# Handing the multiplications of a 31-tap depthwise convolution from GpSimd to ScalarE

## The chip, the cores and the metric

The kernel runs on one core of one Trainium2 chip. The metric is the device time of one execution in microseconds (us). The program has five engines that work from queues of their own: TensorE (PE in the profile; PEld is its weight load), VectorE (DVE), ScalarE (ACT), GpSimd (POOL) and SyncE (SP, which issues the DMAs).

## The reference, cut to what matters

The model is a stack of two blocks. The second has two layers, each with a "hybrid mixer" that adds two branches. Branch a is a gated delta rule over 4 heads, forward and backward; branch b is a convolution branch:

```
u = cf_val * jax.nn.sigmoid(cf_glu)                            # 512 tokens x 512 channels
u = depthwise_conv_centred(u, cf_conv_w) + cf_conv_b           # 31 taps along the tokens, per channel
u = jax.nn.silu(layer_norm(u, cf_ln_w, cf_ln_b))
y_b = (u * jax.nn.silu(z_b)) @ w_cf_out
gate = jax.nn.sigmoid(gate_lg + gate_b).reshape(bsz, seq, N_BRANCH, D_MODEL)
y = gate[:, :, 0] * y_a + gate[:, :, 1] * y_b
return y @ w_out
```

All of it is float32. A token's output is a sum over 31 neighbours, each times a weight of its channel.

## The kernel before

Activations lie with channels on the 128 partitions and the 512 tokens along the free axis, one tile ("page") of 128x512 for each 128 channels. A GEMM tile is 8 steps k of three 128x512 matmuls each (lines 331, 334, 335: weights and activations are split into a high and a low part), and each weight tile is split first, by ScalarE (line 77, the high part) and VectorE (line 78, the low part).

The hybrid (line 1783) runs three kinds of work at once. The **foreground** is a row of GEMMs in program order: the projections of the four heads (`gdn_proj`), the convolution's input (`cf_proj`, which stores its four tiles `U` to DRAM), 16 gate tiles (line 1872), 4 tiles `zb` (line 1881), then `branch(1)`, which multiplies the convolution's result by `w_cf_out`. The **heads** (`gdn_head`, two at a time, background) are chains of small matmuls: an inverse (`CH.inverse`, lines 705 to 737, with a GpSimd copy at 718, a ScalarE copy at 730, a VectorE transpose at 729 and a VectorE subtraction at 736) and then 8 scan steps (lines 2096 to 2153). The **convolution** (`cf_conv`, background too) goes through the four channel tiles one after another.

What is woven with what is decided while the program is written out. The planner keeps a clock of its own, `K.now`. Each step k of a foreground GEMM calls `tick`, which moves the clock on by 3 x 512 / 2.37 = 648 ns and then lets those background strands emit that are due. A strand yields two numbers: a cost that moves the clock, and a wait, after which, times `LF` = 2.5, it is due again. The convolution yields `0, CVL` with `CVL` = 900, so that its next step is due 2250 ns later. Tile's scheduler then sets each engine's fixed order, with the order of emission as priority; an instruction can be put ahead of an earlier one where its data and its pages are there, except that foreground matmuls and the heads' matmuls are pinned to each other's order.

Two lines decide what follows the foreground (1884 and 1885): while the convolution has steps left, the planner lets the background strands run alone, and no GEMM is emitted.

```
    while any(s[1] is conv for s in K.back):
        K.wait()
    Yb = cf_norm(K, l, zb, U)
```

Behind them come `cf_norm` (layer norm, SiLU and the product with `zb`), `branch(1)` with the heads' remaining steps woven in, and `K.drain()` (line 1900), which again lets the heads run alone until they end. Then `branch(0)`, which needs all four heads, and `add_out`.

In `cf_conv`, a tile's centre tap and bias are one ScalarE instruction (line 1773). Of its 30 side taps, 20 are VectorE `scalar_tensor_tensor` instructions (line 1779: source times weight plus accumulator, all in SBUF). The other 10 (`PT`) go to GpSimd, each as two instructions: a multiplication into the page `x` (line 1945) and an addition into a second accumulator `g` (line 1946). VectorE adds the two accumulators at the end (line 1950).

Of the kernel before, what the change touches and what calls it, by code (L numbers as in the profile page):

```python
# [10 lines left out]
AF = mybir.ActivationFunctionType  # L11
# [3 lines left out]
ADD, SUB, MUL, MAX = ALU.add, ALU.subtract, ALU.mult, ALU.max  # L15
# [1728 lines left out]

CVL = 900
SLG = 1.0
PT = range(1, 31, 3)
HP = 10


# [15 lines left out]
def conv_n(K, dst, src, n, taps, bias=None, skip=()):  # L1766

    nc = K.nc
    c = len(taps) // 2
    if bias is None:  # L1770
        nc.scalar.activation(dst[:, :n], src[:, :n], AF.Copy, scale=taps[c])
    else:
        nc.scalar.activation(dst[:, :n], src[:, :n], AF.Identity, scale=taps[c], bias=bias)  # L1773
    for j in range(len(taps)):
        o = j - c
        if o == 0 or j in skip:
            continue
        a, b = max(0, -o), n - max(0, o)
        nc.vector.scalar_tensor_tensor(dst[:, a:b], src[:, a + o:b + o], taps[j], dst[:, a:b], MUL, ADD)  # L1779
        yield 0, CVL  # L1780


def hybrid(K, CH, l, X):
# [74 lines left out]
    for h in range(2):  # L1858
        proj(h)
        K.background(heads[h], head(h), slow=SLG)  # L1860
    cf_proj(K, l, X, w, U)
    conv = cf_conv(K, l, U)
    K.background(pro, conv)
    for h in range(2, 4):
# [65 lines left out]
def cf_conv(K, l, U):  # L1930

    nc = K.nc
    for t in range(4):
        while len(K.free_pages["p"]) < 4:
            yield 0, 1000
        src = K.load(U[t], "l")
        taps = [K.v(f"cfw{l}", 4 * j + t) for j in range(31)]
        U[t], g = [K.p2(name="cfa") for _ in range(2)]
        x = K.p2(name="tap")
        conv = conv_n(K, U[t], src, LT, taps, K.v(f"cfb{l}", t), PT)  # L1940
        nc.gpsimd.memset(g, 0.0)
        for j in PT:
            o = j - 15
            a, b = max(0, -o), LT - max(0, o)
            nc.gpsimd.tensor_scalar(x[:, a:b], src[:, a + o:b + o], taps[j], None, MUL)  # L1945
            nc.gpsimd.tensor_tensor(g[:, a:b], g[:, a:b], x[:, a:b], ADD)  # L1946
            for _ in range(2):
                yield next(conv, (0, CVL))
        yield from conv
        nc.vector.tensor_tensor(U[t], U[t], g, ADD)  # L1950
        K.free(src, g, x)


def cf_norm(K, l, zb, U):
# [335 lines left out]
```

## Time and profile before

| what | value |
|---|---|
| time, median of 3 runs | 3411.72 us (3407.67 to 3417.12) |
| profiled execution, its own time | 3407.66 us |
| its span, first to last instruction | 3406.0 us |
| mean granted TensorE clock | 0.958 |
| busy share PE / DVE / ACT / POOL | 93% / 62% / 37% / 18% |

The busy shares are means over the whole program; the two hybrid layers lie in about the last 1150 us of the span, and only there does the convolution run. The page's digits for POOL are near zero in most of the program and reach 5 of 10 in the hybrids.

### The profile page before, as it was taken

To read this page: it belongs to the slowest core of one execution; us is meant where nothing else is said; L and a number is where in the kernel's file an instruction comes from. 1 tells how busy PE (TensorE), PEld (TensorE's weight loads), DVE (VectorE), ACT (ScalarE), POOL (GpSimd) and SP (SyncE) were. 2 spreads that over 40 slices of the span, in tenths; PEclk is the share of its full clock that TensorE was granted. 3 is DMA by queue.
4 is the path that set the end of the run, shared out by engine and by line. 5 is a ranking of instruction groups with operands and counts; after the bars stand their busy time and mean duration, and the time that the engine had idled before them with its cause. 6 is when DMAs were issued, how large, how long until landed. Compare 5 with 4: busy or idle time off the path is not lost. (4 is left out here: it accounts for less than half of the span.)

```text
span 3406.0 us, 61963 instructions
## 1 busy us (share of the span) xinstructions
PE 3156.2 (93%) x25042; PEld 2473.4 (73%) x25042; DVE 2114.3 (62%) x4318; ACT 1271.8 (37%) x2681; POOL 624.0 (18%) x762
## 2 busy tenths in 40 slices
PE   7999988889899999989888999989999998899998
PEld 4878766667588888868766788857667676766756
DVE  4444556545855555584766675668578666777765
ACT  4333333333432222355534332352333335244332
POOL 4111223211000000010010000005158100515700
PEclk9999999999899999989999999989999898999989
DMA  7432545441222122222222233232223253223333
GB/s 233 137 94 71 166 148 166 133 124 51 76 72 69 64 79 66 77 66 71 87 66 87 87 100 123 87 100 72 72 90 100 76 174 95 75 69 100 100 118 105
DMA packets 313570, 336.10 MB, mean 99 GB/s; under 512 B 26542, under 2 KB 259132, under 8 KB 313284
## 3 DMA queue, kind: packets, MB, share of 16 engines
q1 hardware_dynamic: 311172, 329.69, 30.6%
q8 instruction: 197, 3.23, 0.4%
q0 software_dynamic: 2112, 2.45, 0.3%
q14 instruction: 89, 0.73, 0.1%
HBM read 282.13 MB, written 49.94 MB: 97 GB/s over the span
## 5 line engine op out<-in xcount | busy, mean ns | idle before, releaser
L331 PE MATMUL mm<-hl,wh 128*128 128x512 f32 (+1 forms) x3296 | 1252.2, 384 | 53.8 <-DVE qkv L1779 13.8
L334 PE MATMUL mm<-hl,wh 128*128 128x512 f32 (+1 forms) x3296 | 1223.6, 372 | 1.9 <-DVE hl L474 1.6
L335 PE MATMUL mm<-hl,wl 128*128 128x512 f32 (+1 forms) x3296 | 1215.9, 371 | 0.0
L331 PEld LDWEIGHTS mm<-hl,wh 128*128 128x128 f32 x3296 | 629.6, 192 | 194.8 <-issue 40.4
L335 PEld LDWEIGHTS mm<-hl,wl 128*128 128x128 f32 x3296 | 630.3, 191 | 114.0 <-issue 2.3
L334 PEld LDWEIGHTS mm<-hl,wh 128*128 128x128 f32 x3296 | 632.2, 192 | 104.9 <-DVE hl L474 4.0
L77 ACT ACTIVATE wh<-wr 128x512 fp32r<-128x512 f32 (+3 forms) x718 | 367.4, 561 | 698.1 <-PE mm L334 610.9
L78 DVE TENSOR_TENSOR wl<-wr,wh 128x512 fp32r<-128x512 f32 (+3 forms) x718 | 438.3, 644 | 213.6 <-ACT wh L77 196.8
L1357 DVE SCALAR_TENSOR_TENSOR cv<-mm,vecs,cv 128x441 f32<-128x441 f32 (+2 forms) x352 | 243.0, 692 | 94.2 <-ACT cv L1345 88.1
L1408 POOL MEMSET gwh<- 128x1024 f32 x3 | 2.9, 955 | 971.3 <-PE mm L334 971.3
L1779 DVE SCALAR_TENSOR_TENSOR cfa<-ld,vecs,cfa 128x497 f32<-128x497 f32 (+14 forms) x160 | 154.3, 964 | 18.3 <-ACT cfa L1773 16.1
L1945 POOL TENSOR_SCALAR tap<-ld,vecs 128x498 f32<-128x498 f32 (+4 forms) x80 | 150.7, 1883 | 46.7 <-DVE kq L2004 10.4
L1380 DVE TENSOR_TENSOR fy<-fy,mm 128x512 f32<-128x512 f32 x96 | 55.1, 576 | 126.3 <-PE mm L335 125.5
L1946 POOL TENSOR_TENSOR cfa<-cfa,tap 128x498 f32<-128x498 f32 (+4 forms) x80 | 113.0, 1413 | 5.3
L2121 ACT ACTIVATE u<-ps,beT 64x128 f32<-64x128 f32 x128 | 46.3, 362 | 137.1 <-DVE u L2120 136.1
L730 ACT ACTIVATE pad<-ps 128x256 f32<-128x256 f32 (+1 forms) x100 | 46.6, 467 | 129.9 <-PE ps L726 129.4
L1359 ACT ACTIVATE cv<-cv,vecs 128x256 f32<-128x256 f32 (+1 forms) x66 | 43.0, 653 | 132.1 <-DVE cv L1357 77.2
L736 DVE TENSOR_TENSOR cut<-cut,ps 128x256 f32<-128x256 f32 x120 | 49.4, 413 | 58.9 <-PE ps L735 57.2
L353 POOL TENSOR_TENSOR rs<-var,mhalf 128x4 f32<-128x4 f32 (+1 forms) x26 | 28.1, 1082 | 287.5 <-DVE var L351 287.4
L412 PE MATMUL ps<-sq,one 128*128 128x512 f32 (+1 forms) x132 | 64.5, 625 | 17.0 <-ACT sq L382 15.7
L1363 DVE TENSOR_TENSOR cv<-cv,mm 128x512 f32<-128x512 f32 x66 | 39.4, 599 | 65.5 <-ACT cv L1359 36.2
L2120 DVE TENSOR_SCALAR u<-ps,kdT 64x128 f32<-64x128 f32 x128 | 44.6, 348 | 52.9 <-PE ps L2116 44.5
(479 smaller groups left out, 4465.3 us busy)
## 6 DMA issues: line engine op xcount, KB each, us to landing
ar<-in_ada_w_dram SPq DMA_DIRECT2D x96, 512.0 KB
wr<-in_ffn_up_dram SPq DMA_DIRECT2D x44, 1024.0 KB
wr<-in_w_in_dram SPq DMA_DIRECT2D x28, 1024.0 KB
ld<-sp SPq DMA_DIRECT2D x84, 256.0 KB
wr<-in_w_in_dram SPq DMA_DIRECT2D x32, 512.0 KB
xsp<-x SPq DMA_DIRECT2D x48, 256.0 KB
x<-xsp SPq DMA_DIRECT2D x48, 256.0 KB
wr<-in_ffn_down_dram SPq DMA_DIRECT2D x20, 512.0 KB
```

The source lines that it names most:

```text
L77: nc.scalar.activation(h[:, q:e], src, AF.Copy)
L78: nc.vector.tensor_tensor(l[:, q:e], src, h[:, q:e].bitcast(F32), SUB)
L331: mm = nc.tensor.matmul(ps[:m, :n], wh[:, i, :m], H[:, :n], start=first and i == 0, stop=False)
L334: nc.tensor.matmul(ps[:m, :n], wh[:, i, :m], L[:, :n], start=False, stop=False)
L335: nc.tensor.matmul(ps[:m, :n], wl[:, i, :m], H[:, :n], start=False, stop=last and i == nk - 1)
L412: self.nc.tensor.matmul(ps[:, :n], self.one2, t[:, :n], start=first, stop=last)
L736: nc.vector.tensor_tensor(Wp, Wp, ps, SUB)
L1357: nc.vector.scalar_tensor_tensor(t3[:, ro, co], a3[:, ri, ci], tap(ky, kx, ff), t3[:, ro, co], MUL, ADD)
L1380: nc.vector.tensor_tensor(y[s][q], y[s][q], pss[s][:, :n], ADD)
L1779: nc.vector.scalar_tensor_tensor(dst[:, a:b], src[:, a + o:b + o], taps[j], dst[:, a:b], MUL, ADD)
L1945: nc.gpsimd.tensor_scalar(x[:, a:b], src[:, a + o:b + o], taps[j], None, MUL)
L1946: nc.gpsimd.tensor_tensor(g[:, a:b], g[:, a:b], x[:, a:b], ADD)
```

## The change

The set of taps on GpSimd's side becomes every second one, 16 of 30 instead of 10; VectorE keeps the other 14. For each of the 16, ScalarE multiplies (an activation with `Copy` and the weight as scale) into one of two pages used in turn, and GpSimd only adds. The inner loop yields once for each of the 16, where it yielded twice for each of 10. A tile needs five free pages to begin instead of four, since there is one page more for products.

```
-PT = range(1, 31, 3)
+PT = range(0, 31, 2)
...
-        while len(K.free_pages["p"]) < 4:
+        while len(K.free_pages["p"]) < 5:
...
-        x = K.p2(name="tap")
+        xs = [K.p2(name="tap") for _ in range(2)]
...
-        for j in PT:
+        for i, j in enumerate(PT):
             o = j - 15
             a, b = max(0, -o), LT - max(0, o)
-            nc.gpsimd.tensor_scalar(x[:, a:b], src[:, a + o:b + o], taps[j], None, MUL)
+            x = xs[i % 2]
+            nc.scalar.activation(x[:, a:b], src[:, a + o:b + o], AF.Copy, scale=taps[j])
             nc.gpsimd.tensor_tensor(g[:, a:b], g[:, a:b], x[:, a:b], ADD)
-            for _ in range(2):
-                yield next(conv, (0, CVL))
+            yield next(conv, (0, CVL))
...
-        K.free(src, g, x)
+        K.free(src, g, *xs)
```

## Rows read from the trace of the kernel before

**Rows 1.** The page's part 1: busy us, share of the span, instructions.

```profile
PE 3156.2 (93%) x25042; PEld 2473.4 (73%) x25042; DVE 2114.3 (62%) x4318; ACT 1271.8 (37%) x2681; POOL 624.0 (18%) x762
```

**Rows 2.** Busy time by stretch: length, each engine's busy us, PEclk, DMA share, GB/s.

```profile
2338.00:2390.00 52.00, 44.64 (x571) 35.73 (x571) 45.79 (x51) 12.58 (x22) 43.40 (x27) 0.93 0.14 42
2482.00:2522.00 40.00, 34.96 (x159) 22.97 (x159) 31.73 (x61) 11.01 (x26) 35.43 (x23) 0.91 0.18 60
2589.00:2649.00 60.00, 55.42 (x718) 42.48 (x717) 44.04 (x63) 17.69 (x35) 45.28 (x30) 1.00 0.27 85
2682.00:2711.60 29.60, 23.59 (x128) 14.22 (x127) 21.09 (x57) 13.08 (x35) 2.63 (x3) 0.60 0.22 67
2711.60:2752.60 41.00, 39.85 (x174) 28.02 (x173) 20.82 (x55) 10.02 (x30) 1.10 (x2) 0.96 0.63 207
3258.50:3287.50 29.00, 22.63 (x130) 13.99 (x130) 21.39 (x58) 13.42 (x36) 1.31 (x2) 0.65 0.23 70
```

**Rows 3.** The same stretches, line 331's instructions alone: PE, PEld, PEclk, DMA, GB/s.

```profile
2682.00:2711.60 29.60, 0.00 (x0) 0.00 (x0) 0.60 0.22 67
2711.60:2752.60 41.00, 17.95 (x41) 8.07 (x41) 0.96 0.63 207
3258.50:3287.50 29.00, 0.00 (x0) 0.00 (x0) 0.65 0.23 70
```

**Rows 4.** PE's timeline at the end of layer 0's last head.

```profile
2742.54 0.43 PE L2143 MATMUL ps<-u,at 64*64 64x128 f32 x2
...
2750.57 0.60 PE L2171 MATMUL ps<-ident,ot 128*128 128x128 f32 x4
```

**Rows 5.** Groups by line, hybrids: busy us, mean ns | idle before, releasers.

```profile
L1779 DVE SCALAR_TENSOR_TENSOR cfa<-ld,vecs,cfa 128x497 f32<-128x497 f32 (+14 forms) x160 | 154.3, 964 | 18.3 <-ACT cfa L1773 16.1
...
L1945 POOL TENSOR_SCALAR tap<-ld,vecs 128x498 f32<-128x498 f32 (+4 forms) x80 | 150.7, 1883 | 46.7 <-DVE kq L2004 10.4 <-PE mm L335 10.3 <-DMA sp<-gt 6.8
L1946 POOL TENSOR_TENSOR cfa<-cfa,tap 128x498 f32<-128x498 f32 (+4 forms) x80 | 113.0, 1413 | 5.3
L718 POOL TENSOR_TENSOR pad<-L,zm 128x512 f32<-128x512 f32 x40 | 59.2, 1485 | 62.3 <-PE ps L726 47.4 <-ACT L L2081 14.7
```

**Rows 6.** Line 1779 by its instructions: duration ns min/median/max, first and last start.

```profile
L1779 DVE SCALAR_TENSOR_TENSOR cfa<-ld,vecs,cfa x160: 695/745/1823, 2339.4 to 3193.0; 128x497 f32<-128x497 f32 x16, 128x500 f32<-128x500 f32 x16, 128x503 f32<-128x503 f32 x16, 128x506 f32<-128x506 f32 x16
L1779 DVE SCALAR_TENSOR_TENSOR qkv<-mm,vecs,qkv x96: 714/748/752, 2266.5 to 3057.3; 128x510 f32<-128x510 f32 x48, 128x511 f32<-128x511 f32 x48
```

**Rows 7.** DVE's timeline in layer 0's first and second tile: start, us.

```profile
2340.01 0.69 DVE L78 TENSOR_TENSOR wl<-wr,wh 128x512 fp32r<-128x512 f32 x1
2340.61 1.75 DVE L1779 SCALAR_TENSOR_TENSOR cfa<-ld,vecs,cfa 128x499 f32<-128x499 f32 x1
2342.28 1.77 DVE L78 TENSOR_TENSOR wl<-wr,wh 128x512 fp32r<-128x512 f32 x1
...
2486.06 1.53 DVE L1779 SCALAR_TENSOR_TENSOR cfa<-ld,vecs,cfa 128x506 f32<-128x506 f32 x2
```

**Rows 8.** POOL's timeline at the same two places, and its last tap of layer 0.

```profile
2340.29 1.54 POOL L1946 TENSOR_TENSOR cfa<-cfa,tap 128x498 f32<-128x498 f32 x1
2341.78 1.72 POOL L718 TENSOR_TENSOR pad<-L,zm 128x512 f32<-128x512 f32 x1
...
2485.08 1.86 POOL L1945 TENSOR_SCALAR tap<-ld,vecs 128x501 f32<-128x501 f32 x1
...
2647.67 1.26 POOL L1946 TENSOR_TENSOR cfa<-cfa,tap 128x499 f32<-128x499 f32 x1
```

**Rows 9.** DVE's weight splits of 128x512 in the hybrids, by form.

```profile
L78 DVE TENSOR_TENSOR wl<-wr,wh 128x512 fp32r<-128x512 f32 x204 | 157.4, 801 | 63.8 <-ACT wh L77 59.8 <-PE ps L2038 3.6
```

**Rows 10.** ACT's groups by form in the hybrids.

```profile
L1773 ACT ACTIVATE cfa<-ld,vecs,vecs 128x512 f32<-128x512 f32 x8 | 6.5, 816 | 19.9 <-DMA ld<-sp 13.3 <-DMA sp<-gt 5.1 <-DVE kq L2004 1.5
...
L382 ACT ACTIVATE sq<-cfa 128x512 f32<-128x512 f32 x8 | 4.6, 619 | 0.0
```

**Rows 11.** What PE waited for, 2335 to 2400 us: total, times, longest.

```profile
PE ps L726 <- DVE W L736: 7.4, 3, 5.3
```

## The prediction

> **What bounds the kernel now.** First the page's part 1 [rows 1]: TensorE is busy 93% of the span and GpSimd 18%. So time saved on GpSimd is worth nothing in itself; the question is where TensorE waits in the hybrids, and whether that wait hangs on the convolution. Second, busy time by stretch [rows 2]. The first three rows are three of the stretches in which GpSimd works on taps in layer 0: PE is idle 52.0 - 44.6 = 7.4, 5.0 and 4.6 us, 17 in sum, while DVE is busy 45.8 of 52, 31.7 of 40 and 44.0 of 60. Layer 1 repeats the code, so I count 34 us in two layers. The waits view names it in the first stretch [rows 11]: the inverse's matmul (726) waits for VectorE's subtraction (736), queued behind taps and weight splits. Third, the rows of 2682.0 to 2711.6 and 3258.5 to 3287.5: PE is busy 23.6 of 29.6 us at a granted clock of 0.60, and 22.6 of 29.0 at 0.65. Line 331 alone shows why [rows 3]: not one foreground matmul ran there. This is the planner's loop at lines 1884 and 1885: zb's GEMMs are out, the convolution has planned steps left, so only the heads run, on latencies. On the chip the convolution's last GpSimd tap starts at 2647.67 and takes 1.26 us [rows 8], so it is done 33 us before this hole begins: the hole comes from the written-out order, not from data. In full-clock work it holds 23.59 x 0.60 = 14.2 us, so 15.4 of 29.6 are lost; in layer 1, 22.63 x 0.65 = 14.7, so 14.3. Together **29.7 us** hang on when the planner thinks that the convolution ends.
>
> **The change part by part.** All counts are for two layers, eight tiles.
>
> *VectorE's taps.* 160 become 112. At their mean of 964 ns [rows 5] that is -46.3 us of VectorE; but the same instruction fed from PSUM, which never met GpSimd, takes 714 to 752 [rows 6]. At 741, inside that, 48 taps are -35.6; the other 223 ns x 160 = 35.7 us are something else.
>
> *That something else is GpSimd's addition.* A tap that starts 0.3 us into an addition takes 1.75 us, and the split behind it, which meets the copy of line 718, 1.77 [rows 7, 8]: each starts its real work when the two-input GpSimd instruction is through. Under a GpSimd multiplication (2485.08, 1.86 us) two taps took 1.53 together, 0.77 each: almost undisturbed. So it is the additions that cost VectorE, and these go from 80 to 128, while the harmless multiplications go. Measured per addition: 35.7 / 80 = 0.45 us of tap time. Bounds for one addition: nothing, where VectorE works from PSUM at that moment, and 1.75 - 0.74 = 1.0. I keep 0.45, the mean over all tiles: 128 x 0.45 = 57.6, against 35.7 now: +21.9. Splits pay too: 801 ns in the mean [rows 9] against 0.69 us for an undisturbed one [rows 7], 0.11 x 204 = 22 us over 120 two-input GpSimd instructions (80 additions, 40 copies); with 168 it is 9 more. VectorE in sum: -35.6 + 21.9 + 9 = **-5 us**, hardly a relief; with no further collision -36, with 1.0 for each addition about +66.
>
> The Trainium skill (SBUF — State Buffer, "Who interferes with whom") says that a VectorE instruction with two SBUF inputs contends with any GpSimd instruction that reads SBUF, and that the pair is locked for the whole instruction. The rows agree for additions and not for the one-input multiplication. By the rule the contention would follow GpSimd's whole tap time, which falls; that is a rival below.
>
> *GpSimd.* -80 x 1.883 = -150.7, +48 x 1.413 = +67.8: tap time 263.7 becomes 181 us, 22.6 a tile instead of 33 [rows 5]. Off the path; the 40 copies of line 718 that stand in the same queue get shorter waits, unless an addition ahead of them waits for its product.
>
> *ScalarE.* +128 multiplications, 128x497 and wider, from SBUF with a scale per partition. No such row: from below 619 ns (a square from SBUF, no scale), from above 816 (scale and bias per partition, from SBUF) [rows 10]. I take 0.70, nearer the square, since the bias falls away: +90 us (79 to 104), 11.2 a tile. Cover: ScalarE is busy 12.6 of 52, 11.0 of 40 and 17.7 of 60 in these stretches [rows 2]. What it costs all the same: each ScalarE instruction that meets a multiplication under way waits half of 0.70; with 11.2 us in about 40 that is 0.1 us apiece. These stretches hold 22 + 26 + 35 of them per layer, perhaps a quarter on a head's chain: 2 us a layer, **+4**. Bounds: 0, and 2 x 83 x 0.1 = 17. The new wait is that multiplication i+2 needs the page that addition i frees; behind it in ScalarE's queue stand the high splits (77), the copies 730 and the scan's u (2121). With additions at 1.4 us and products at 0.7 ScalarE is the faster one and would wait, if the order were not fixed with room between. No DMA is added; the loads of tiles 1 to 3 are only issued earlier.
>
> *Pages.* Five free instead of four. Followed through the code's bookkeeping, 14, 8, 10 and 9 pages are free where the tiles begin, so the gate costs nothing.
>
> *The planner.* The part that I think decides. Each layer now plans 4 x 20 = 80 convolution steps, at least 2.25 us apart, each rounded up to the next foreground step of 0.648 (half a step in the mean: 2.57): 206 us; stepped through, the code's clock gives 209. Foreground from the convolution's start to zb's end: 28 GEMM tiles x 8 x 0.648 = 145 us, plus the heads' own costs, 41 in that stretch: 186. The convolution outlasts it by 23, and that is the hole. After: 4 x 16 = 64 steps, 64 x 2.6 = 167 us, under 186. The loop has nothing to wait for; `branch(1)` follows zb directly and covers the heads' steps that now run alone. The heads are not shortened: what they have left then runs alone in the drain, two scan steps and the output of the last head. That costs, from rows: from the last scan matmul to the transposes 8.0 us [rows 4], and two steps at 29.6 / 5 = 5.9 (five steps of each head ran in the hole), 20 in sum. In it TensorE can do some 9 steps k of `branch(0)` that do not need the last heads: the second stretch has 41 [rows 3] where `branch(1)` has 32. They are 9 x 0.69 = 6.2 us; the steps' own matmuls are about 3. So 11 are lost there, where 15.4 + 41.0 - 39.85 x 0.96 = 18.1 are lost now: -7 in layer 0, -6 in layer 1 with its smaller hole, **-13**. Bounds: 0 (the hole moves whole) and -29.7.
>
> *When taps run.* The four tiles take 167 of planned time, not 209, so the inverse of heads 2 and 3 is about half clear of them (4.6 us idle in the third stretch: -2.3), and the scan's crowded stretch has 6 taps fewer of 20 (5.0 idle x 6/20 = -1.5). Two layers: **-8** (0 to -10, which is 34 x 6/20).
>
> Sum against the profile's own 3407.66 (span 3406.0 and 1.7 around it): -13 - 8 + 4 = -17, so 3390.7. The median stands 4.1 above that execution, so **3395** for it. VectorE's -5 is inside the -8.
>
> **The rivals.** (a) *The hole is only moved*: the heads alone at the end cost what they cost now, at a low clock. For it: their chain is unchanged. Then -8 + 4 remains: 3408, within the bound of 0.3% (10 us), about what these runs can tell from nothing. (b) *Additions crowd VectorE*: at 0.9 us each, which back-to-back additions make likely where VectorE is 88% busy already [rows 2], the taps cost 128 x 0.9 - 35.7 - 35.6 = +44 and the splits +9, 53 us of VectorE; if half reaches TensorE, 26 - 13 + 4 = +17: 3429, slower. It decides from a collision of 0.63, where half of 128 x 0.63 - 71.3 + 9 = 18 eats the 9 that hole and ScalarE leave. Against it: in the scan most VectorE operands come from PSUM. (c) *Contention falls with GpSimd's tap time*: if any GpSimd work on taps held VectorE up alike, collisions would be 35.7 x 181 / 263.7 = 24.5, so taps fall from 154.3 to 83 + 24.5 = 107.5, -30%; the 34 us of idle lose as much or a little more, 13, and the hole gives 20: 3383. Against it stand the undisturbed taps of [rows 7, 8]. It is what the section of the Trainium skill named above would give.
>
> **How the numbers follow.** Forecast 0.42 (3383 to 3405), (a) 0.20, (b) 0.25, (c) 0.13. Faster by over 0.3% (under 3401.5): most of the forecast, 0.36, all of (c), 0.02 of (a): 0.51. Slower: 0.25, from (b). Same: 0.24. The range takes in (c) and its bounds below and (b) above: 3374 to 3428.
>
> **What would show it.** Right: line 331 runs on past zb without the gap, a shorter gap stands ahead of `branch(0)`, line 1946 has 128 at 1.4 to 1.6 us, line 1779's taps a mean near 1.25, ScalarE's multiplications 0.62 to 0.82. Wrong: taps near 1.75 and longer waits of line 726 for 736 (b); a gap as long as now, elsewhere (a); taps under 1.0 (c); or idle time of ScalarE in front of the new line that ends with GpSimd, with splits and copies late behind it.

## The result: slower by 31 us, and the profile after

The changed kernel takes 3441.0 us (median of 6 runs, 3437.54 to 3452.2) against 3410.31 us for the kernel before (6 runs beside it, 3407.54 to 3417.12): ratio 1.0095, 95% interval 1.0078 to 1.0112. That is 31 us slower; 17 us faster was forecast.

The profiled execution of after has a span of 3450.5 us, 44.5 more than before's 3406.0. Of these, 9.7 stand ahead of the first hybrid layer, where the order is unchanged (its first `qkv` instruction comes at 2272.6 instead of 2262.9), so they are not the change's. Layer 0 is 18.8 longer (574.5 to 593.3 us from its first `qkv` to that of layer 1) and layer 1 16.0 (568.6 to 584.6, to the end).

The page's part 1 of after, as [rows 1]:

```profile
PE 3171.2 (92%) x25042; PEld 2480.6 (72%) x25042; DVE 2097.4 (61%) x4270; ACT 1357.2 (39%) x2810; POOL 537.2 (16%) x730
```

VectorE and GpSimd are both less busy than before (-16.9 and -86.8 us), and the kernel is slower: the sums can't tell why. The groups of after, as [rows 5] (busy us, mean ns | idle before, releasers); ScalarE's products are line 1946 now and GpSimd's additions line 1947:

```profile
L1947 POOL TENSOR_TENSOR cfa<-cfa,tap 128x497 f32<-128x497 f32 (+7 forms) x128 | 184.1, 1438 | 97.5 <-ACT tap L1946 91.2
...
L1779 DVE SCALAR_TENSOR_TENSOR cfa<-ld,vecs,cfa 128x498 f32<-128x498 f32 (+6 forms) x112 | 110.0, 982 | 17.6 <-ACT cfa L1773 16.0
...
L1946 ACT ACTIVATE tap<-ld,vecs 128x497 f32<-128x497 f32 (+7 forms) x128 | 90.6, 713 | 89.3 <-POOL cfa L1947 55.9 <-DMA sp<-gt 22.3 <-DMA ld<-sp 9.1
```

The waits of after in the hybrids (engine, line waited for: total us, times, longest):

```profile
POOL cfa L1947 <- ACT tap L1946: 91.2, 26, 8.9
...
ACT tap L1946 <- POOL cfa L1947: 55.9, 61, 2.0
...
PE ps L726 <- DVE W L736: 31.8, 9, 5.3
...
PE ps L2171 <- DVE ot L2166: 16.9, 4, 6.2
```

Before, the same view has one of the four:

```profile
PE ps L726 <- DVE W L736: 23.2, 12, 5.4
```

So TensorE waits 8.6 us more for the inverse's subtraction on VectorE, and 16.9 us for something that it did not wait for before: the heads' output, scaled by VectorE (2166) before its transpose (2171).

Where the 35 us of the two layers lie, is told by busy time by stretch (length, then busy us of PE, PEld, DVE, ACT, POOL, granted clock, DMA share, GB/s). The first two rows run from the convolution's start to the end of `zb` in layer 0 and 1; the other three are layer 0 from `zb`'s end to the first step of `branch(1)`, to its last, and to the output of the last head. Before:

```profile
2338.50:2682.70 344.20, 321.07 (x2743) 235.56 (x2741) 255.74 (x444) 121.38 (x247) 171.51 (x112) 0.97 0.26 81
2913.50:3259.50 346.00, 318.93 (x2743) 233.92 (x2741) 254.81 (x443) 121.02 (x246) 171.84 (x112) 0.97 0.26 80
2682.70:2717.80 35.10, 29.01 (x144) 17.95 (x144) 22.87 (x65) 12.67 (x34) 2.73 (x3) 0.61 0.17 49
2717.80:2744.60 26.80, 26.61 (x121) 18.34 (x120) 14.99 (x36) 8.60 (x28) 0.26 (x1) 1.00 0.76 256
2744.60:2751.20 6.60, 6.60 (x32) 5.23 (x30) 2.41 (x8) 0.55 (x2) 0.75 (x1) 1.00 0.75 238
```

After:

```profile
2348.50:2708.00 359.50, 324.50 (x2745) 236.77 (x2743) 245.94 (x420) 162.51 (x311) 129.08 (x97) 0.95 0.24 76
2942.00:3299.40 357.40, 322.51 (x2745) 236.43 (x2743) 246.98 (x420) 162.25 (x311) 129.95 (x97) 0.95 0.24 76
2708.20:2722.20 14.00, 9.40 (x30) 6.01 (x31) 8.63 (x18) 6.67 (x14) 0.00 (x0) 0.63 0.31 104
2722.20:2757.10 34.90, 34.08 (x184) 22.10 (x184) 22.04 (x62) 10.50 (x35) 1.66 (x2) 1.00 0.56 186
2757.10:2777.80 20.70, 15.43 (x78) 9.12 (x78) 9.59 (x29) 4.28 (x16) 1.01 (x1) 0.79 0.48 146
```

Two things are to be seen. In the first two rows the same TensorE work (2745 instructions, 2743 before) takes 716.9 us instead of 690.2, 26.7 more: PE idles 69.9 us instead of 50.2, and is busy 7.0 longer at a granted clock of 0.95 instead of 0.97, between the levels of 1.2 and 2.4 GHz (1.0 is 2.4). And the hole behind `zb` did shrink, 35.1 to 14.0, but `branch(1)`, which now has the heads' steps woven in, grew by 8.1, and the wait behind it by 14.1: 68.5 us before, 69.6 after. To the end of its layer it is 154.7 us from `zb`'s end in layer 0 and 146.5 in layer 1 before, and 157.9 and 151.1 after: 7.8 more in sum, where 13 fewer were forecast. One wait has about that size. Its line is the same in both (in the hybrids, before and then after):

```profile
PE mm L331 <- ACT hl L311: 1.8, 2, 1.5
```

```profile
PE mm L331 <- ACT hl L311: 10.5, 4, 4.4
```

The first matmul of `branch(1)` needs the result of `cf_norm`, split by ScalarE (311). Before, that chain ran in the hole, beside the heads; now it comes right behind `zb`, and TensorE waits 4.42 us for it in each layer. In the stretch ahead of the last head's output line 331 stands still from 2763.7, as it did in the hole of [rows 3] (line 331 alone, in the same columns up to PEld, then clock, DMA share, GB/s):

```profile
2763.70:2779.30 15.60, 0.03 (x1) 0.03 (x1) 0.67 0.24 71
3353.70:3370.60 16.90, 0.00 (x0) 0.00 (x0) 0.67 0.37 109
```

How TensorE comes to wait ahead of `zb`'s end is on the timelines (start, us, instruction). VectorE of after in the first tile, and GpSimd beside it:

```profile
2352.43 1.77 DVE L78 TENSOR_TENSOR wl<-wr,wh 128x512 fp32r<-128x512 f32 x1
2354.13 1.72 DVE L1779 SCALAR_TENSOR_TENSOR cfa<-ld,vecs,cfa 128x502 f32<-128x502 f32 x1
2355.78 1.77 DVE L78 TENSOR_TENSOR wl<-wr,wh 128x512 fp32r<-128x512 f32 x1
2357.47 5.05 DVE L1779 SCALAR_TENSOR_TENSOR cfa<-ld,vecs,cfa 128x504 f32<-128x504 f32 x3
2362.45 0.68 DVE L736 TENSOR_TENSOR W<-W,ps 128x512 f32<-128x512 f32 x1
...
2353.61 10.03 POOL L1947 TENSOR_TENSOR cfa<-cfa,tap 128x501 f32<-128x501 f32 x6
```

Six additions stand back to back, 1.67 us each, and six VectorE instructions with two inputs from SBUF (the first still beside a copy of line 718) run at their pace, 1.68 to 1.77 each instead of about 0.7. In before a multiplication stands between two additions, and a tap that starts beside it is hardly held up: counted over the whole trace of before, the 45 taps that start during a GpSimd multiplication take 746 ns in the median (844 in the mean), the 44 that start during a two-input GpSimd instruction 1639 (1426), and the 66 that start while GpSimd is idle 740 (753). The subtraction (736) that TensorE waits for is behind all six. The same in the third tile, where it hits the output of head 1; VectorE, then TensorE:

```profile
2553.57 4.09 DVE L1779 SCALAR_TENSOR_TENSOR cfa<-ld,vecs,cfa 128x508 f32<-128x508 f32 x3
2557.58 1.74 DVE L78 TENSOR_TENSOR wl<-wr,wh 128x512 fp32r<-128x512 f32 x1
2559.24 1.75 DVE L1779 SCALAR_TENSOR_TENSOR cfa<-ld,vecs,cfa 128x502 f32<-128x502 f32 x1
2560.92 1.76 DVE L78 TENSOR_TENSOR wl<-wr,wh 128x512 fp32r<-128x512 f32 x1
2562.60 1.50 DVE L1779 SCALAR_TENSOR_TENSOR cfa<-ld,vecs,cfa 128x500 f32<-128x500 f32 x2
2564.13 0.60 DVE L2149 TENSOR_TENSOR ot<-ot,ps 64x128 f32<-64x128 f32 x2
...
2568.61 1.48 DVE L2166 TENSOR_SCALAR ot<-ot,ors 128x128 f32<-128x128 f32 x2
...
2563.30 0.40 PE L335 MATMUL mm<-hl,wl 128*128 128x512 f32 x1
2569.95 0.47 PE L2171 MATMUL ps<-ident,ot 128*128 128x128 f32 x1 [6.25 <-DVE ot L2166]
```

TensorE's last matmul of the head (2143) began at 2558.17, but VectorE takes its result (2149) up only at 2564.13, behind the row of taps and splits. The head's output also passes through GpSimd (line 2163), but GpSimd stood idle for 3.32 us in front of it, waiting for VectorE.

Taps and splits are not the only ones that are held up. The heads have VectorE instructions with two inputs from SBUF too; line 2049, before, after, and in e4 (the experiment below that gives GpSimd's instruction one input):

```profile
L2049 DVE TENSOR_TENSOR qd<-qd,kq 128x256 f32<-128x256 f32 x32 | 11.9, 421 | 2.9 <-DMA qd<-sp 2.7
```

```profile
L2049 DVE TENSOR_TENSOR qd<-qd,kq 128x256 f32<-128x256 f32 x32 | 20.2, 678 | 5.2 <-DMA qd<-sp 5.2
```

```profile
L2049 DVE TENSOR_TENSOR qd<-qd,kq 128x256 f32<-128x256 f32 x32 | 12.0, 424 | 9.9 <-DMA qd<-sp 9.9
```

### The profile page after: what moved, and what is told of

Read it like the earlier page. It is cut to its first block, busy times and chain, and to the rows that moved or that the text cites. A ratio compares the mean times of both kernels' runs of the same rounds, so it can differ in the third digit from the quotient of the medians.

```text
span 3450.5 us, 62092 instructions
## 1 busy us (share of the span) xinstructions
PE 3171.2 (92%) x25042; PEld 2480.6 (72%) x25042; DVE 2097.4 (61%) x4270; ACT 1357.2 (39%) x2810; POOL 537.2 (16%) x730
## 3 DMA queue, kind: packets, MB, share of 16 engines
q1 hardware_dynamic: 311172, 329.69, 29.7%
## 4 chain that ended last, share of the span: by engine, by line
PE 74%; DVE 13%; ACT 5%; DMA 3%; issue 3%; POOL 2%; SPq 0%; DVEq 0%; POOLq 0%; ACTq 0%
PE mm L331 19%; PE mm L334 17%; PE mm L335 17%; PE ps L1177 2%; PE ps L726 2%; PE ps L735 2%; DVE cfa L1779 2%; DVE wl L78 2%; PE ps L1122 1%; PE ps L545 1%; POOL cfa L1947 1%; PE ps L1704 1%; PE ps L412 1%; DMA ar<-in_ada_w_dram 1%; PE ps L2143 1%
## 5 line engine op out<-in xcount | busy, mean ns | idle before, releaser
L78 DVE TENSOR_TENSOR wl<-wr,wh 128x512 fp32r<-128x512 f32 (+3 forms) x718 | 445.6, 654 | 223.6 <-ACT wh L77 212.6
L1947 POOL TENSOR_TENSOR cfa<-cfa,tap 128x497 f32<-128x497 f32 (+7 forms) x128 | 184.1, 1438 | 97.5 <-ACT tap L1946 91.2
L1380 DVE TENSOR_TENSOR fy<-fy,mm 128x512 f32<-128x512 f32 x96 | 55.2, 577 | 126.3 <-PE mm L335 125.5
L1946 ACT ACTIVATE tap<-ld,vecs 128x497 f32<-128x497 f32 (+7 forms) x128 | 90.6, 713 | 89.3 <-POOL cfa L1947 55.9
L1779 DVE SCALAR_TENSOR_TENSOR cfa<-ld,vecs,cfa 128x498 f32<-128x498 f32 (+6 forms) x112 | 110.0, 982 | 17.6 <-ACT cfa L1773 16.0
L2120 DVE TENSOR_SCALAR u<-ps,kdT 64x128 f32<-64x128 f32 x128 | 44.6, 349 | 71.3 <-PE ps L2116 55.2
L412 PE MATMUL ps<-sq,one 128*128 128x512 f32 (+1 forms) x132 | 62.9, 609 | 17.3 <-ACT sq L382 15.5
```

What stands on the lines that cost most here:

```text
L78: nc.vector.tensor_tensor(l[:, q:e], src, h[:, q:e].bitcast(F32), SUB)
L412: self.nc.tensor.matmul(ps[:, :n], self.one2, t[:, :n], start=first, stop=last)
L1946: nc.scalar.activation(x[:, a:b], src[:, a + o:b + o], AF.Copy, scale=taps[j])
```

## The experiments

Four causes could make the conv-to-`zb` stretch longer: the two-input additions, now closer together (collisions); ScalarE's and GpSimd's queues, which wait for each other 91.2 and 55.9 us; the written-out order; and the place of the taps ahead of the heads' instructions. A ratio is to the kernel before, run on the same chip; before's medians on the four chips used lie between 3408.25 and 3411.49 us, so that times of two experiments compare to some 3 us.

**Collisions or queues.** e4 keeps after's products, pages and yields, and gives GpSimd's instruction one input instead of two. The taps are then not summed, so this is a probe and no replacement; the same holds for e5, e13 and e14.

```
-            nc.gpsimd.tensor_tensor(g[:, a:b], g[:, a:b], x[:, a:b], ADD)
+            nc.gpsimd.tensor_scalar(g[:, a:b], x[:, a:b], 1.0, None, MUL)
```

> The changed kernel, but GpSimd's addition is a one-input multiplication by 1 of the product into the accumulator's page, so that it reads one SBUF operand (the 16 taps are not summed: the output leaves them out, all but the last one). Collisions: the taps of line 1779 fall to about 760 ns and the time to 3405 to 3415. Order: 3441 +-5. Queues: the instruction is as long as the addition (1.55 to 1.9 us), so products wait as long or longer, 3436 to 3450.

Measured: 3393.89 us, ratio 0.9951 [0.9936, 0.9966]; 47 us under after, 0.5% under before, and below all three forecasts. Its groups, waits, and the two conv-to-`zb` stretches:

```profile
L1947 POOL TENSOR_SCALAR cfa<-tap 128x497 f32<-128x497 f32 (+7 forms) x128 | 202.8, 1584 | 88.0 <-ACT tap L1946 75.9 <-DMA E<-sp 6.4
...
L1779 DVE SCALAR_TENSOR_TENSOR cfa<-ld,vecs,cfa 128x498 f32<-128x498 f32 (+6 forms) x112 | 94.8, 846 | 18.7 <-ACT cfa L1773 17.0
```

```profile
POOL cfa L1947 <- ACT tap L1946: 75.9, 27, 7.9
...
ACT tap L1946 <- POOL cfa L1947: 52.8, 44, 3.2
...
PE ps L726 <- DVE W L736: 9.8, 4, 3.8
...
PE ps L2171 <- DVE ot L2166: 7.5, 4, 2.8
```

```profile
2344.50:2676.30 331.80, 316.89 (x2745) 231.52 (x2743) 215.50 (x420) 161.85 (x311) 140.31 (x97) 0.98 0.27 83
2912.00:3244.60 332.60, 316.15 (x2744) 232.24 (x2743) 216.45 (x420) 161.13 (x311) 137.68 (x97) 0.98 0.27 82
```

GpSimd is busy longer (202.8 us against 184.1), the two queues wait for each other about as long as in after, and all the same TensorE's two waits fall from 48.7 to 17.3 us, its idle time in the stretches from 69.9 to 31.4, and they are 52.5 us shorter. So the queues fall as a cause. Counted by what GpSimd does at their start, e4's taps take 897 ns in the mean beside a one-input instruction (49 taps) and 737 beside an idle GpSimd (52); after's take 1514 beside a two-input one (35). But the edit does not change the instruction alone. Tile's scheduler also gives another order: of VectorE's instructions in the hybrids, 93% stand in one common order in the traces of after and e4. What that moves is a part of the 47 us that e4 can't separate; e13, below, does better.

e5 makes the same edit to the 80 additions of before.

> The kernel before with its 80 additions on GpSimd as one-input multiplications by 1 into the accumulator's page (the 10 taps are not summed: the output leaves all but the last of them out). Collisions: the kernel before paid for them too, 0.45 us each on line 1779 and the splits: some 20 us less, 3385 to 3398. Order: no change, 3411 +-6.

3408.79 us, 0.9996 [0.9986, 1.0006]: nothing, though the taps fall from 964 to 890 ns and TensorE's wait for 736 from 23.2 to 16.5 us. The collisions of before cost no time that could be won back in this way.

**ScalarE's part alone.** e1 moves only the multiplication, for before's 10 taps:

```
-PT = range(0, 31, 2)
+PT = range(1, 31, 3)
...
-            yield next(conv, (0, CVL))
+            for _ in range(2):
+                yield next(conv, (0, CVL))
```

> ScalarE multiplies, but GpSimd keeps 10 taps of 30 and the planner its 20 steps a tile. Collisions (VectorE held up by GpSimd's additions, dense after the change): the additions are 80 as before, though closer together; 3410 to 3422. Order (the shorter plan): as before, 3410 +-5. Queues (products wait for page and addition, additions for products, and heads' work stands behind both): 80 of 128 products, so some 60% of the +31, 3425 to 3432.

3438.52 us, 1.009 [1.0073, 1.0106]: above all three forecasts, and nearly all of the loss, with before's 80 additions. e13 gives e1 the one-input edit.

> e1_act_mult_10 with GpSimd's 80 additions replaced by one-input multiplications by 1.0 (the products are not summed). The order stays that of e1. If e1's 27 us are two-input additions that meet VectorE's two-input instructions: 3390 to 3405. If ScalarE's 80 products or the order cost them: 3430 to 3440.

3396.19 us, 0.9962 [0.9949, 0.9975]. The groups of e1 (1533 ns for each addition), and then of e13, and of both the wait of TensorE:

```profile
L1779 DVE SCALAR_TENSOR_TENSOR cfa<-ld,vecs,cfa 128x497 f32<-128x497 f32 (+14 forms) x160 | 160.8, 1005 | 15.6 <-ACT cfa L1773 13.2
L1947 POOL TENSOR_TENSOR cfa<-cfa,tap 128x498 f32<-128x498 f32 (+4 forms) x80 | 122.6, 1533 | 48.5 <-ACT tap L1946 44.6
L726 PE MATMUL ps<-W,pad 64*64 64x64 f32 x1280 | 50.1, 234 | 33.9 <-DVE W L736 33.9
```

```profile
L1779 DVE SCALAR_TENSOR_TENSOR cfa<-ld,vecs,cfa 128x497 f32<-128x497 f32 (+14 forms) x160 | 138.6, 866 | 16.0 <-ACT cfa L1773 13.5
L1947 POOL TENSOR_SCALAR cfa<-tap 128x498 f32<-128x498 f32 (+4 forms) x80 | 132.0, 1650 | 52.3 <-ACT tap L1946 48.4
L726 PE MATMUL ps<-W,pad 64*64 64x64 f32 x1280 | 46.5, 226 | 12.8 <-DVE W L736 12.8
```

Here the order hardly moves: 98% of VectorE's instructions stand in one common order in e1 and e13, as many as in after and e7 (below), which differ by a PSUM bank alone. So ScalarE's 80 products cost nothing that shows, and the second input of GpSimd's additions costs 42 us of e1. The number of additions is not what decides: 80 lose as much as 128. In before, where a multiplication stands between two additions, the same edit (e5) gives nothing. That the multiplication between them is what makes the difference is read from the rows; no run puts one back and leaves the rest as it is.

**Taps out of SBUF, and the place of the first tile.** e6 lets VectorE accumulate in a PSUM bank (its taps then have one input from SBUF), which leaves the foreground two banks; e7 is after with two banks alone.

```
+    pro.mm = deque([0, 1])
     conv = cf_conv(K, l, U)
...
+    pro.mm = deque([0, 1, 2])
     Yb = cf_norm(K, l, zb, U)
...
+        acc = K.psum.tile([P, 512], F32, tag="b2", bufs=1, name=K.nm("cacc"))
-        conv = conv_n(K, U[t], src, LT, taps, K.v(f"cfb{l}", t), PT)
+        conv = conv_n(K, acc, src, LT, taps, K.v(f"cfb{l}", t), PT)
...
-        nc.vector.tensor_tensor(U[t], U[t], g, ADD)
+        nc.vector.tensor_tensor(U[t], acc, g, ADD)
```

> The changed kernel, but VectorE's accumulator lies in a PSUM bank (taken from the foreground's three), so that a tap reads only one operand from SBUF; additions, products and planner stay. Collisions: taps of line 1779 back to about 745 ns, the splits of line 78 still held up: 3395 to 3415. Order, or waits in ScalarE's and GpSimd's queues: 3435 to 3450.

> The changed kernel with the foreground on two PSUM banks instead of three while the convolution runs, accumulator in SBUF: what the bank alone costs. All theories: 3441 to 3450.

e6: 3405.88 us, 0.9991 [0.9981, 1.0]. e7: 3442.68 us, 1.0102 [1.0087, 1.0117]. Two banks cost nothing, the accumulators bring 37 us. But this edit does two things: the scheduler gives tile 0 its bank later, so that VectorE's first tap comes at 2386.6 us in e6 and at 2340.7 in e7, behind the crowded end of the first inverse. e15 keeps that late start and the two banks, and puts the taps back into SBUF:

```
+        first = dst if acc is None else acc
+        nc.scalar.activation(first[:, :n], src[:, :n], AF.Identity, scale=taps[c], bias=bias)
+        if acc is not None:
+            nc.scalar.activation(dst[:, :n], acc[:, :n], AF.Copy)
...
-        conv = conv_n(K, U[t], src, LT, taps, K.v(f"cfb{l}", t), PT)
+        conv = conv_n(K, U[t], src, LT, taps, K.v(f"cfb{l}", t), PT, acc)
```

> The accumulators of e6_after_psum_acc in PSUM also move VectorE's taps of tile 0 some 40 us later, behind the last steps of the first inverse. This kernel keeps that move alone: the first value of the accumulator is written to the same PSUM bank and copied by ScalarE to SBUF at once (8 copies more), where VectorE's taps accumulate as in after, with two inputs from SBUF. If e6's 37 us are the collisions of the taps: 3430 to 3445, as e7. If they are the later start of tile 0: 3400 to 3415. Half of each: near 3425.

3426.69 us, 1.005 [1.0033, 1.0067]. The taps of e7, of e15 (line 1782 there) and of e6, min/median/max in ns, first and last start:

```profile
L1779 DVE SCALAR_TENSOR_TENSOR cfa<-ld,vecs,cfa x112: 694/746/1781, 2340.7 to 3189.3; 128x498 f32<-128x498 f32 x16, 128x500 f32<-128x500 f32 x16, 128x502 f32<-128x502 f32 x16, 128x504 f32<-128x504 f32 x16
```

```profile
L1782 DVE SCALAR_TENSOR_TENSOR cfa<-ld,vecs,cfa x112: 698/741/1787, 2383.4 to 3174.9; 128x498 f32<-128x498 f32 x16, 128x500 f32<-128x500 f32 x16, 128x502 f32<-128x502 f32 x16, 128x504 f32<-128x504 f32 x16
```

```profile
L1779 DVE SCALAR_TENSOR_TENSOR cacc<-ld,vecs,cacc x112: 705/741/754, 2386.6 to 3171.5; 128x498 f32<-128x498 f32 x16, 128x500 f32<-128x500 f32 x16, 128x502 f32<-128x502 f32 x16, 128x504 f32<-128x504 f32 x16
```

About half and half: of the 37 us, 16 come from tile 0's later place alone and 21 from taps that no longer meet additions (the longest tap is 754 ns, not 1787). In e15 the wait for 736 falls to 10.6 us, while the one for the head's output stays at 16.6: each belongs to one place.

The same accumulators under before (e8) and under e1 (e9):

> The kernel before with VectorE's accumulator in that PSUM bank. Collisions: its 35.7 us of held-up taps go, some 10 to 18 us of the path: 3393 to 3402, faster than both kernels. Order: 3411 to 3420, the bank's cost.

> e1_act_mult_10 (10 GpSimd taps as before, multiplied on ScalarE) with VectorE's accumulator in a PSUM bank, foreground matmuls on two banks while the convolution runs. If e1's 27 us over before are VectorE taps that take turns with the dense GpSimd additions: most of them come back, 3400 to 3412, taps at 0.74. If they come from ScalarE's 80 products or from the order of the program: it stays at 3430 to 3440.

e8: 3399.04 us, 0.9977 [0.9963, 0.9991]. e9: 3394.78 us, 0.9965 [0.9952, 0.9978], 44 under e1. Tile 0 starts late in both of these too (its centre tap on ScalarE at 2383.5 and 2387.3 us, against 2338.5 in before and in e1), so that they do not tell the start's share from the taps'. e9 is the fastest version that still computes the reference, 15 us under before.

**The plan.** The planner's wait `CVL` sets how closely the steps follow each other. e2 is before with 720 (its 20 steps in about the planned time of 16), e14 adds the one-input edit, e10 the accumulators; e3 is after with 1125 (16 steps in the time of 20), e11 is e6 and e12 is e8 with 1125.

```
-CVL = 900
+CVL = 720
```

> The kernel before with 20 planner steps a tile of 1.8 us in place of 2.25 (CVL 720), so that the convolution ends in the plan about where the changed kernel's does; engines as before. Order: like the changed kernel, 3430 to 3441. Collisions, queues: the engines' work is that of before, 3410 +-6.

> e2_before_short_plan with GpSimd's 80 additions replaced by one-input multiplications by 1.0 (the products are not summed). The order stays that of e2. If e2's 47 us are collisions: 3400 to 3420. If the order costs them (taps ahead of what the heads need): 3440 or more.

> e2_before_short_plan (before with CVL = 720, the same engines' work, 47 us slower) with VectorE's accumulator in a PSUM bank. If the short plan loses because it packs taps and additions more densely so that they meet: back to 3400 to 3420. If it loses by the written-out order (taps placed ahead of what the heads need, for a VectorE that is full with or without collisions): 3435 or more stays.

e2: 3458.7 us, 1.0144 [1.0129, 1.0159], above both forecasts. e14: 3433.13 us, 1.0067 [1.0049, 1.0084]. e10: 3421.56 us, 1.004 [1.0025, 1.0055]. Neither theory holds alone: of 47 us lost with no engine's work changed, about 26 go with the second input, and 25 remain (e10, against e8: 23). So the closer plan costs in the order as well; by what wait was not found.

> The changed kernel with 16 planner steps a tile of 2.81 us (CVL 1125), so that the convolution's planned length is that of before; engines as changed. Order: back to 3410 +-6. Collisions, queues: still 3430 to 3441, a little less if spreading the additions helps.

> e6_after_psum_acc (3405.9) with CVL = 1125, which spreads the 16 steps of a tile over the time that 20 took. If what is left over e4's 3394 is density of the steps on VectorE and ScalarE: faster, 3390 to 3400. If the heads' chain alone sets the layer's end and collisions are gone already: 3400 to 3412, no change.

> e8_before_psum_acc (3399) with CVL = 1125: 20 steps a tile, spread over a quarter more planned time. If density on VectorE is what the short plan paid for: a little faster, 3385 to 3398. If the longer hole behind zb costs more than that: 3400 to 3425.

e3: 3442.3 us, 1.0097 [1.0082, 1.0112]; line 331's gap behind `zb` is back (30.2 and 29.7 us), and the time is that of after, as two differences of the traces cancel: from the convolution's start to `zb`'s end e3's two layers take 13 us less than after's (352.1 and 351.7 us), behind `zb` 8 more (162.6 and 154.8). e11: 3411.67 us, 1.0003 [0.9989, 1.0016], no better than e6. e12: 3418.34 us, 1.0037 [1.0023, 1.0051], with gaps of 55.2 and 54.6 us, 19 over e8: from the start of their layers to `zb`'s end its two layers take 3 us less (818.3 for 821.5), and behind it 25 more (330.0 for 305.1). So a longer gap does cost, and in e3 the shorter stretch ahead of it makes up for that.

## Why the prediction was wrong

**The hole (forecast -13).** This step failed: behind `zb` the two layers take 7.8 us more, not 13 less. Rival (a) had the mechanism: the hole was moved. The planner's loop had nothing to wait for, as worked out, and a shorter gap (15.6 and 16.9 us) stands ahead of `branch(0)`. But `branch(1)` does not follow `zb` directly: 14.0 us lie between them, since `cf_norm`, which the forecast put at nothing, stands there (TensorE's two waits of 4.42 us). The arithmetic also left out that the heads' woven-in steps lengthen `branch(1)` (26.8 to 34.9), and it let some 9 steps of `branch(0)` fill the drain: line 331 shows one instruction there. From `zb`'s end to the last head's output it is 68.5 us before, 69.6 after, and 69.7 in e4 and e6 as well, which end at quite different times. In these four the heads' chain sets that length; the gap only shows where they run alone.

**The taps' timing (forecast -8, VectorE -5 inside it).** This step failed in sign: 26.7 us lost in the conv-to-`zb` stretches instead of 8 won. VectorE's sum was even better than forecast (16.9 us less busy on the page, -5 forecast): all taps take 110.0 us (140.6 forecast), 982 ns in the mean instead of 1.25 us; above 741 that is 27.0 us, 0.21 for each of 128 additions, not 0.45. The splits of the hybrids pay 7 us (181.9 to 189.0; 9 forecast). The heads' own two-input instructions, such as line 2049 (421 to 678 ns), the forecast left out. What I priced was a mean over all tiles; what counts is the row. With no multiplication between them the additions make VectorE's two-input instructions take turns, at 1.7 us, up to six in a row, just where 736 and the heads' output stand behind them. The one-input edit takes 42 us back in e13, with nearly the same order, and 47 in e4, where some of the order changes too. One reading of the rows was too kind: of the two taps of 1.53 us at 2486.06 only the first ran inside the multiplication, which ended at 2486.94; the second was under way when the next addition began. The count over all taps bears the reading out all the same.

**The rivals.** (b) had the direction and the mechanism, back-to-back additions where VectorE is busy already, and forecast 3429 (just outside the range of 3374 to 3428 that was to take it in); but its own measure, 0.63 per addition and taps near 1.75, was not reached (0.21): what decides is not a mean per addition. (c) has the taps' sum nearly exactly, 107.5 for 110.0, and is refuted twice: the time went the other way, and in e4 GpSimd's tap time rises while the taps fall to 94.8. The rule in the Trainium skill's "SBUF — State Buffer" ("Who interferes with whom") is that any GpSimd instruction that reads SBUF contends with a VectorE instruction that has two inputs from SBUF. It fits in part: beside a one-input GpSimd instruction e4's taps take 897 ns where an idle GpSimd leaves 737, but beside a two-input one after's take 1514, though the two are about equally long (1584 and 1438 ns).

**ScalarE (forecast +4).** The price was right (0.713 us, 0.70 forecast). The waits that would show it wrong did come (91.2 and 55.9 us between the two queues), and cost nothing visible: e4 has them too and is faster than before, e9 with 80 products on ScalarE is no slower than e8 without.

**The rest.** Additions 1.438 us (1.4 to 1.6) and GpSimd's tap time 184.1 (181) came as worked out. That the gate of five pages costs nothing no run shows by itself; the plan ended ahead of `zb`, as it would with the gate open.

Left open: how much of e4's 47 us the other order brings, why the collisions of before cost nothing (e5), why the closer plan alone costs some 24 us without collisions, and how much more could be had by placing the taps elsewhere (e15 shows that one tile's place is worth 16 us).

## What to carry to other kernels

Price a contention by its rows, not by its mean: ask which instructions stand one after another on both engines, and what waits behind them; an instruction that stands between two contending ones can be what lets the other engine through, as the rows here suggest. Before counting a gap as lost time, find the chain that ends last behind it: if that chain is as long without the gap, the gap only moves. And ask what the gap hid: what ran in it stands in the open once it is closed, as `cf_norm` does here. Where two engines contend for SBUF, look at the number of operands first: here an accumulator in PSUM or one operand less was worth more than a shorter instruction.

## What the hardware showed that was not expected

The second input decides most of it. A one-input GpSimd instruction on the same pages, longer by itself (1584 ns against 1438), leaves VectorE's taps at 846 ns and TensorE's two waits at 17.3 us; the two-input one gives 982 ns and 48.7 us. And taps that accumulate in PSUM do not see the additions at all (705 to 754 ns in e6), while splits, which stay in SBUF, still do: VectorE's splits of the hybrids take 184.4 us in e6 and 165.1 in e4.
